# Hybrid decoder block on one core: the output projection's second and third chained products run one branch group later, the sums of activations come on every second step, and the second resident weight tile is asked for later

## The chip, the cores and the metric

The kernel runs on one core of one Trainium2 chip. The metric is the device time of one execution in microseconds (us); lower is better. The time before is 1326.16 us, the median of 3 runs (1325.57 to 1326.43).

## What is computed

One decoder block over 256 tokens of width 2048: an input projection, a dilated-window attention branch and a gated-MLP branch, a gated merge of the two, an output projection, a layer norm, a feed-forward layer of width 8192 and a second layer norm. The change touches the stage between the two branches and the output projection:

```python
y_a = jnp.einsum('bse,ed->bsd', attn, w_proj_a)
y_b = jnp.einsum('bse,ed->bsd', gmlp, w_proj_b)
merged = jax.nn.sigmoid(ga) * y_a + jax.nn.sigmoid(gb) * y_b
return jnp.einsum('bsd,de->bse', merged, w_out)
h = layer_norm(ALPHA * h + mix, ln1_gain[layer], ln1_bias[layer])
```

## The kernel before, in words

**Weights and precision.** Every weight matrix is read once, as chunks of 512 rows by 512 columns (1 MB, a `raw` tile of 4 x 512 per partition; three such buffers, loads issued from SP, L145). A chunk is used in two **pieces** of 128 x 1024. Each piece is split into a rounded part `hi` (a copy on ACT, L188) and a remainder `lo` (a subtraction on DVE, L157); TensorE (PE) multiplies with both. When the `lo` of a chunk's last piece has been written, the load of the chunk three places on is issued (L162).

**Steps.** The program is a list of steps in the order in which PE does them, one piece to a step. Six split buffers (the ring) hold pieces ahead of PE: at the emission of step s (`emit_splits`, L170; loop at L979) the split of the piece of step s + 5 is issued, into the buffer that step s - 1 has just left. So on ACT and DVE, which work in the order of issue, a split stands five steps ahead of its matmuls. In each step the order of issue is: the split; the hi and lo of finished activations (`rounds`); one or two pending finishing operations (`later`); the step's matmuls and, at the end of a group, its evacuations; then what `at` has hung on that step.

**Groups.** `pa` and `pb` are the branch groups: 512 columns of `w_pa` or `w_pb`, four steps each ("ws" mode, L252 and L254). At the end of one, four halves are copied from PSUM on ACT (`halves`, L273) and added on DVE (L277). After pb, DVE multiplies and adds for the gated merge (L486, L489), and hi and lo of the merged activations follow (L93, L94). "as" groups (L240 to L242) are quarters of the output projection in plain form, two steps to a chunk.

**Products.** For half of the output projection's columns, seven products P1 to P7 over 512 x 512 blocks take the place of eight ("sum" mode, L212 to L214, two steps of six matmuls each; the results are added up in `collect`, L684). Four of them use a **resident tile** that stays in SBUF: the first (`tiles["b", 0]`) is loaded once and, after each of P1, P5 and P6, changed in place: when the `lo` of the product's second piece is written, `held_add` (L632) issues from POOL a DMA that adds another weight block to it. So P1, P5, P6 and P4 are chained. The second resident tile (`tiles["b", 1]`, used by P7) is made by `held_load(uo, 1)` (L620): a plain load from POOL (L623) and, once that has landed, a DMA that adds a second block (L625). It lies on the buffer `A1`, which the merged activations of group 1 hold until the sums below have read them. Each such DMA moves 1 MB, and POOL issues its DMAs in program order.

**Sums of activations.** P5, P6, P7 and P3 take sums and differences of activations. `sum_of_acts` (L567) makes them in four parts k = 0 to 3: four DVE operations into `cb` (L575 to L578), then hi and lo (`ca`, L93 and L94) in the next step's `rounds`. P5's second step needs parts 2 and 3.

**The order around the change** (L844 to L861): pa0 pb0 pa1 pb1 pa2 P1 pb2 P5 pa3 P6 pb3, then the plain group of columns 1024 to 1535 in four chunks c0 to c3 with products between them: c0 P7 c1 P4 c2 P3 c3 P2. The sums are hung on P1's second step and the three steps that follow it; `held_load(uo, 1)` on P5's first step. After pb3, `start_residual` (L496) issues two loads of 1 MB from POOL, the residual rows `y`.

In the texts below, step 0 is the first step of pb2. The steps before the change are then: pb2 0 to 3, P5 4 and 5, pa3 6 to 9, P6 10 and 11, pb3 12 to 15, c0 16 and 17, P7 18 and 19, c1 20 and 21, P4 22 and 23. "P7a" and "P7b" are the first and second piece of P7, and so on for others.

Of the kernel before, what the change touches and what calls it, by code (L numbers as in the profile page):

```python
# [26 lines left out]
G = 8  # L27
# [44 lines left out]
def block_kernel(ctx: ExitStack, tc: tile.TileContext, xT, x, w_in, rel_bias, lnv_g, lnv_b, wsT, b_sp,  # L72
# [25 lines left out]
    chunks, pieces, steps = [], [], []  # L98
# [30 lines left out]
    def add_step(piece, part, first=False, last=False):  # L129
        pieces[piece]["uses"] += 1  # L130
        steps.append((piece, part, first, last))
        return len(steps) - 1

    def add_group(g, sizes=None):
        hs = add_pieces(g, sizes)
        for h in hs:
            add_step(h, "all", h == hs[0], h == hs[-1])
# [162 lines left out]
    tiles = {}  # L300
# [171 lines left out]
    def ev_ya(g):  # L472
        def fin(ot, s):
            gt = tiles["G", g]
            nc.vector.tensor_tensor(gt[:, 0, ot, :], gt[:, 0, ot, :], s, op=ALU.mult)

        def ev(ot, p):
            later.append((fin, ot, halves(p)))
        return ev

    def ev_yb(g):
        def fin(ot, s):
            if g == 0 and ot == 0:
                tiles["merged"] = quads("merged", [f"S1{i}" for i in range(4)])
            gt, d = tiles["G", g], tiles["merged"][g][:, ot, :]
            nc.vector.tensor_tensor(s, s, gt[:, 1, ot, :], op=ALU.mult)  # L486

            q = kept(ot) if g == 0 else gt[:, 0, ot, :] if g == 1 else s
            nc.vector.tensor_tensor(q, s, gt[:, 0, ot, :], op=ALU.add)  # L489
            rounds.append((hilo, d[:, :S], d[:, S:], q))  # L490

        def ev(ot, p):
            later.append((fin, ot, halves(p)))
        return ev
# [72 lines left out]
    def sum_of_acts(tags, ot, q):  # L567


        if ot == 0:  # L570
            for i in range(2):
                tiles["ca", i] = big.tile([P, 2, NCT, 2, P], F32R, name="ca", tag=tags[i])
        q0, t0, t1 = tiles["q", ot], slice(0, P), slice(P, S)
        cb = work.tile([P, 4, P], F32, name="cb", tag="pt")
        nc.vector.tensor_tensor(cb[:, 0], q0[:, t1], q[:, t1], op=ALU.subtract)  # L575
        nc.vector.tensor_tensor(cb[:, 2], q0[:, t0], q0[:, t1], op=ALU.subtract)
        nc.vector.tensor_tensor(cb[:, 1], cb[:, 0], q0[:, t0], op=ALU.subtract)
        nc.vector.tensor_tensor(cb[:, 3], q[:, t0], cb[:, 1], op=ALU.add)  # L578
        for i in range(2):
            d = tiles["ca", i][:, :, ot]  # L580
            rounds.append((hilo, d[:, :, 0], d[:, :, 1], cb[:, 2 * i:2 * i + 2]))
# [34 lines left out]
    def out_unit():  # L616
        return SimpleNamespace(w=w_out, row=0, act=lambda r, k: tiles["merged"][r][:, k, :],
                               tags=("S5", "A1"), acc="A0", key="out", scale=ALPHA)
# [176 lines left out]
    def quad(key):  # L795
        return lambda k: tiles[key][k // 4][:, k % 4, :]
# [5 lines left out]
    def at(s, f, *a):  # L802
        side.setdefault(s, []).append((f, a))
# [32 lines left out]
    uo = out_unit()  # L836
    prods = products(uo)

    def add_product(name):
        hs = prods[name]()  # L840
        for h in hs:
            add_step(h, "all", h == hs[0], h == hs[-1])

    at(len(steps) + 8, held_load, uo, 0)  # L844
    for i in range(4):
        add_group(Group(w_pa, i * CW, 8, quad("attnT"), "ws", ev_ya(i)))
        if i >= 2:
            add_product(("P1", "P6")[i - 2])
        if i == 2:
            for k in range(4):  # L850
                at(len(steps) - 1 + k, lambda k=k: sum_of_acts(("S6", "W"), k, tiles["G", 1][:, 0, k, :]))
        add_group(Group(w_pb, i * CW, 8, quad("gmlpT"), "ws", ev_yb(i), after=start_residual if i == 3 else None))
        if i == 2:
            at(len(steps), held_load, uo, 1)
            add_product("P5")

    g = Group(w_out, 2 * CW, 16, quad("merged"), "as", ev_out(2))
    for c, name in enumerate(("P7", "P4", "P3", "P2")):
# [169 lines left out]
```

## Time and profile before

| | before |
|---|---|
| median of 3 runs | 1326.16 us |
| the profiled execution's own time | 1326.2 us |
| its span | 1324.5 us |
| PE busy | 1312.9 us (99%) |
| DVE busy | 939.0 us (71%) |
| ACT busy | 691.0 us (52%) |
| POOL busy | 51.7 us (4%) |
| DMA | 288.83 MB, mean 218 GB/s |
| mean granted TensorE clock | 0.998 of full |

The profiled execution took 1326.2 us, 1.7 us more than its span, the time that the trace covers. An engine is busy when an instruction of it runs; matmuls are pipelined, so a matmul's listed duration (0.39 us for 512 columns) is longer than the distance to the next one (0.23 us). In a timeline a bracket at the end of a row gives the idle time of the engine just before it and what ended it.

### The profile page before, as it was taken

How to read it: one execution, taken by the hardware profiler on the slowest of the kernel's cores; microseconds unless marked ns; L12 is line 12 of the kernel's file. 1: busy time of each engine (PE TensorE's matmuls, PEld its weight loads, DVE VectorE, ACT ScalarE, POOL GpSimd, SP SyncE). 2: the span in 40 equal slices, each digit the busy share in tenths (PEclk: the TensorE clock that was granted, in tenths of full speed). 3: DMA queues.
4: the chain of work that ended last, by engine and by line, in shares of the span. 5: the costliest groups of instructions: out<-in, count | busy, mean ns of one | idle time of the engine just before them, and what ended most of it. 6: DMA issues, size and time to landing. Idle time of an engine off the chain costs nothing. (4 is left out here: it accounts for less than half of the span.)

```text
span 1324.5 us, 17423 instructions
## 1 busy us (share of the span) xinstructions
PE 1312.9 (99%) x6832; PEld 1111.0 (84%) x6832; DVE 939.0 (71%) x1426; ACT 691.0 (52%) x938; POOL 51.7 (4%) x57
## 2 busy tenths in 40 slices
PE   9999999999999999999999999999999999999998
PEld 6888888888888888889888888888888888888886
DVE  6554678565545689788769768678677796786776
ACT  4444465454544556545545366455555564555641
POOL 0000000000000001000000100010000000100000
PEclk9999999999999999999999999999999999999999
DMA  9866545546555569772874988987887879978561
GB/s 321 289 195 206 176 137 182 191 160 222 191 191 190 187 169 291 244 230 71 283 255 148 284 219 289 248 242 247 217 280 229 237 242 251 252 224 236 178 254 64
DMA packets 140003, 288.83 MB, mean 218 GB/s; under 512 B 5256, under 2 KB 7824, under 8 KB 139024
## 3 DMA queue, kind: packets, MB, share of 16 engines
q1 hardware_dynamic: 120592, 240.26, 53.5%
q0 software_dynamic: 19184, 47.20, 16.8%
q8 instruction: 53, 0.87, 0.3%
q10 hardware_dynamic: 144, 0.26, 0.1%
q14 instruction: 30, 0.25, 0.1%
HBM read 285.59 MB, written 2.11 MB: 217 GB/s over the span
## 5 line engine op out<-in xcount | busy, mean ns | idle before, releaser
L157 DVE TENSOR_TENSOR w<-raw,w 128x1024 fp32r<-128x1024 f32 (+1 forms) x438 | 529.2, 1218 | 300.8 <-ACT w L188 299.7
L188 ACT ACTIVATE w<-raw 128x1024 fp32r<-128x1024 f32 (+1 forms) x438 | 456.7, 1053 | 411.8 <-PE mm L254 289.7
L252 PE MATMUL mm<-hT,w 128*128 128x512 f32 x960 | 339.4, 394 | 0.8 <-DVE sum L277 0.8
L252 PE MATMUL mm<-xs,w 128*128 128x512 f32 x896 | 315.7, 395 | 0.0
L254 PE MATMUL mm<-hT,w 128*128 128x256 f32 x1024 | 276.0, 279 | 0.0
L254 PE MATMUL mm<-xs,w 128*128 128x256 f32 x896 | 250.0, 279 | 0.0
L252 PEld LDWEIGHTS mm<-hT,w 128*128 128x128 f32 x960 | 180.0, 187 | 44.3 <-DVE sum L277 1.1
L252 PEld LDWEIGHTS mm<-xs,w 128*128 128x128 f32 x896 | 167.9, 187 | 39.5
L254 PEld LDWEIGHTS mm<-hT,w 128*128 128x128 f32 x1024 | 188.0, 188 | 2.7
L254 PEld LDWEIGHTS mm<-xs,w 128*128 128x128 f32 x896 | 168.0, 187 | 0.2
L242 PE MATMUL mm<-w,a 128*128 128x512 f32 (+1 forms) x328 | 128.1, 390 | 0.0
L241 PE MATMUL mm<-w,a 128*128 128x512 f32 (+1 forms) x328 | 128.0, 390 | 0.0
L240 PE MATMUL mm<-w,a 128*128 128x512 f32 (+1 forms) x328 | 127.8, 390 | 0.0
L157 DVE TENSOR_TENSOR w<-held,w 128x1024 fp32r<-128x1024 f32 x70 | 85.6, 1223 | 39.3 <-ACT w L188 38.9
L188 ACT ACTIVATE w<-held 128x1024 fp32r<-128x1024 f32 x70 | 73.9, 1058 | 64.7 <-PE mm L242 26.6
L240 PEld LDWEIGHTS mm<-w,a 128*128 128x128 f32 x328 | 61.8, 188 | 14.3
L242 PEld LDWEIGHTS mm<-w,a 128*128 128x128 f32 x328 | 61.7, 188 | 14.0
L241 PEld LDWEIGHTS mm<-w,a 128*128 128x128 f32 x328 | 61.8, 188 | 13.9
L240 PE MATMUL mm<-w,xs 128*128 128x512 f32 x120 | 49.4, 412 | 0.3 <-ACT w L188 0.3
L241 PE MATMUL mm<-w,xs 128*128 128x512 f32 x120 | 47.7, 397 | 1.3 <-DVE w L157 1.3
L277 DVE TENSOR_TENSOR sum<-mm,half 128x256 f32<-128x256 f32 x136 | 48.9, 418 | 0.0
L242 PE MATMUL mm<-w,xs 128*128 128x512 f32 x120 | 47.6, 397 | 0.0
(193 smaller groups left out, 1512.8 us busy)
## 6 DMA issues: line engine op xcount, KB each, us to landing
raw<-in_w_ff_dram SPq DMA_DIRECT2D x116, 1024.0 KB, 6.5
raw<-in_w_in_dram SPq DMA_DIRECT2D x68, 1024.0 KB, 5.1
held<-in_w_ff_dram POOLq DMA_DIRECT2D x36, 1024.0 KB, 8.5
raw<-in_w_out_dram SPq DMA_DIRECT2D x14, 1024.0 KB, 5.4
raw<-in_w_pa_dram SPq DMA_DIRECT2D x8, 1024.0 KB, 5.1
raw<-in_w_pb_dram SPq DMA_DIRECT2D x8, 1024.0 KB, 5.1
held<-in_w_out_dram POOLq DMA_DIRECT2D x6, 1024.0 KB, 8.5
raw<-in_w_in_dram SPq DMA_DIRECT2D x6, 512.0 KB, 7.2
```

The source lines that it names most:

```text
L157: nc.vector.tensor_tensor(h["lo"], sl, f32(h["hi"]), op=ALU.subtract)
L188: nc.scalar.activation(h["hi"], source(h), AF.Copy)
L240: nc.tensor.matmul(p, ah, hi[:, kk, cs], start=first and kk == 0, stop=False)
L241: nc.tensor.matmul(p, ah, lo[:, kk, cs], start=False, stop=False)
L242: nc.tensor.matmul(p, al, hi[:, kk, cs], start=False, stop=last and kk == n - 1)
L252: nc.tensor.matmul(p, hi[:, kk, ws_], av, start=st, stop=False)
L254: nc.tensor.matmul(p[:, :S], lo[:, kk, ws_], av[:, :S], start=False, stop=en)
L277: nc.vector.tensor_tensor(s, p[:, :S], t, op=ALU.add)
```

## The change

The order becomes pa2 P1 pb2 pa3 P5 pb3 P6, then c0 P7 c1 P4 c2 P3 c3 P2 as before: P5 moves behind pa3 and P6 behind pb3. The sums of activations are hung on P1's second step (step -1) and on steps 1, 3 and 5. `held_load(uo, 1)` is issued at step 11, the second step of pb3. The steps after the change: pb2 0 to 3, pa3 4 to 7, P5 8 and 9, pb3 10 to 13, P6 14 and 15, c0 16 and 17, P7 18 and 19. No instruction is added or removed.

```diff
@@ -845,14 +845,14 @@
     for i in range(4):
         add_group(Group(w_pa, i * CW, 8, quad("attnT"), "ws", ev_ya(i)))
         if i >= 2:
-            add_product(("P1", "P6")[i - 2])
+            add_product(("P1", "P5")[i - 2])
         if i == 2:
             for k in range(4):
-                at(len(steps) - 1 + k, lambda k=k: sum_of_acts(("S6", "W"), k, tiles["G", 1][:, 0, k, :]))
+                at(len(steps) - 1 + 2 * k, lambda k=k: sum_of_acts(("S6", "W"), k, tiles["G", 1][:, 0, k, :]))
         add_group(Group(w_pb, i * CW, 8, quad("gmlpT"), "ws", ev_yb(i), after=start_residual if i == 3 else None))
-        if i == 2:
-            at(len(steps), held_load, uo, 1)
-            add_product("P5")
+        if i == 3:
+            at(len(steps) - 3, held_load, uo, 1)
+            add_product("P6")
```

## Rows read from the trace of the kernel before

**Rows 1.** The page: span and part 1, busy time of each engine.
```profile
span 1324.5 us, 17423 instructions
PE 1312.9 (99%) x6832; PEld 1111.0 (84%) x6832; DVE 939.0 (71%) x1426; ACT 691.0 (52%) x938; POOL 51.7 (4%) x57
```

**Rows 2.** Timeline of PE, 498 to 537 us: start, duration, engine, line, operation.
```profile
498.97 0.40 PE L212 MATMUL aux<-w,ca 128*128 128x512 f32 x1
...
502.23 0.50 PE L214 MATMUL aux<-w,ca 128*128 128x512 f32 x1 [0.53 <-DVE ca L94]
502.57 0.40 PE L252 MATMUL mm<-attnT,w 128*128 128x512 f32 x1
...
513.77 0.40 PE L212 MATMUL aux<-w,ca 128*128 128x512 f32 x1
...
533.50 0.40 PE L212 MATMUL aux<-w,ca 128*128 128x512 f32 x1
...
536.31 0.39 PE L240 MATMUL mm<-w,merged 128*128 128x512 f32 x1
```

**Rows 3.** Timeline of DVE, 500 to 508 us.
```profile
500.62 1.22 DVE L157 TENSOR_TENSOR w<-raw,w 128x1024 fp32r<-128x1024 f32 x1
501.76 0.75 DVE L94 TENSOR_TENSOR ca<-cb,ca 128x256 fp32r<-128x256 f32 x2
...
505.45 0.42 DVE L486 TENSOR_TENSOR sum<-sum,gate 128x256 f32<-128x256 f32 x1
...
507.71 0.42 DVE L486 TENSOR_TENSOR sum<-sum,gate 128x256 f32<-128x256 f32 x1
```

**Rows 4.** Timeline of POOL, 493 to 523 us.
```profile
493.25 1.29 POOL L632 DMA_DIRECT2D held<-in_w_out_dram  x1 [14.90 <-DVE w L157]
501.00 0.78 POOL L623 DMA_DIRECT2D held<-in_w_out_dram  x1 [6.47 <-DVE cb L578]
508.07 1.26 POOL L625 DMA_DIRECT2D held<-in_w_out_dram  x1 [6.29 <-DMA held<-in_w_out_dram]
510.02 1.27 POOL L632 DMA_DIRECT2D held<-in_w_out_dram  x1 [0.69 <-DVE w L157]
```

**Rows 5.** Tile held, issues at 493.3, 501.0, 508.1, 510.0: instruction and its landing.
```profile
L632 POOL DMA_DIRECT2D held<-in_w_out_dram x1: 1288/1288/1288, 493.3 to 493.3; - x1
DMA to landing us min/median/max: 8.4/8.4/8.4
...
DMA to landing us min/median/max: 6.8/6.8/6.8
...
DMA to landing us min/median/max: 8.9/8.9/8.9
...
L632 POOL DMA_DIRECT2D held<-in_w_out_dram x1: 1271/1271/1271, 510.0 to 510.0; - x1
DMA to landing us min/median/max: 14.2/14.2/14.2
```

**Rows 6.** Timeline of ACT, 519 to 529 us.
```profile
519.83 1.06 ACT L188 ACTIVATE w<-held 128x1024 fp32r<-128x1024 f32 x1
...
525.25 1.06 ACT L188 ACTIVATE w<-raw 128x1024 fp32r<-128x1024 f32 x1 [1.78 <-PE mm L254]
526.22 0.82 ACT L273 ACTIVATE half<-mm 128x256 f32<-128x256 f32 x2
...
528.36 1.05 ACT L188 ACTIVATE w<-raw 128x1024 fp32r<-128x1024 f32 x1
```

**Rows 7.** Busy time in 502 to 504 us: PE, PEld, DVE, ACT, POOL, clock, DMA, GB/s.
```profile
502.00:504.00 2.00, 1.77 (x10) 1.54 (x11) 1.84 (x6) 1.06 (x2) 0.00 (x0) 1.00 1.07 420
```

**Rows 8.** Timeline of ACT, 767 us (feed-forward stage), a wait for a resident tile.
```profile
767.14 1.06 ACT L188 ACTIVATE w<-held 128x1024 fp32r<-128x1024 f32 x1 [9.84 <-DMA held<-in_w_ff_dram]
```

**Rows 9.** Timeline of PE, 768 to 770 us, the matmuls of that tile.
```profile
768.65 0.39 PE L212 MATMUL aux<-w,ca 128*128 128x512 f32 x1
769.51 0.50 PE L213 MATMUL aux<-w,ca 128*128 128x512 f32 x1 [0.48 <-DVE w L157]
```

**Rows 10.** Tile held, the adding DMA issued at 746.7 us: its landing.
```profile
DMA to landing us min/median/max: 12.5/12.5/12.5
```

**Rows 11.** Busy time in two stretches near the end; columns as in Rows 7.
```profile
1316.00:1318.00 2.00, 0.53 (x2) 0.00 (x0) 1.45 (x3) 1.84 (x6) 0.00 (x0) 1.00 0.00 0
1318.00:1320.00 2.00, 1.35 (x2) 0.30 (x2) 1.94 (x4) 0.53 (x3) 0.00 (x0) 0.82 0.15 59
```

## The prediction

> **What bounds the kernel now.** I read the page first: PE is busy 1312.9 of 1324.5 us [rows 1], so a change that removes no matmul can win only PE's idle time, and any wait that it puts before a matmul is paid in full. Next I read PE's timeline through the stage of the change, where the reader should compare the lengths of like steps. A product is 12 matmuls: P7 runs from 533.50 to 536.31, 2.81 us. P5, the same 12 matmuls, runs from 498.97 to 502.57, 3.60 us [rows 2]. It loses 0.79 us because its last matmul waits for the remainder `ca` of the sums' fourth part. DVE's timeline shows why: it wrote a weight remainder from 500.62 and only then, from 501.76, the last `ca` [rows 3]. Those 0.79 us are all that this stage has to give. Then I read POOL's timeline and the landings, for the tiles that the change moves: each resident tile is a chain of 1 MB DMAs in POOL's order, 6.8 us for the plain load and 8.4 to 14.2 us for an adding one [rows 4, 5].
>
> **The gain.** After the change the fourth part of the sums is hung on step 5 and its `ca` comes in step 6; P5's second step is 9. At 2.81 us a step that is over 7 us of room where there was none, so the wait goes: -0.79 us. The four parts keep their work, now two steps apart. pa3 comes two product steps sooner, its raw loads in the old order three chunks ahead; I cost that at nothing, covered by the five steps of split pieces. Without that cover it would cost what a load is late.
>
> **PE's new timetable, without stalls.** pb2 ends at 498.97 as before. pa3 takes 502.57 to 513.77 = 11.20 us [rows 2], so it ends at 510.17; P5 ends at 512.98; pb3 at 524.18; P6 at 526.99. P7 starts where it did, less the gain: 533.50 - 0.79 = 532.71.
>
> **The first resident tile.** P5b's split goes into the buffer left at 498.97, behind the four halves of pb2. Like those of pb3, where a split starts at 528.36 after halves from 526.22 [rows 6], they take about 2.1 us; with 1.06 for `hi` and 1.22 for `lo` [rows 3, 6] P5's add is issued near 503.8. It lands 8.4 to 8.9 us later [rows 5], near 512.3. P6a's split is due at 511.6 and waits 0.7 us on ACT, which PE, over four steps behind it, does not see. P6b's split needs the buffer that P5 leaves at 512.98; behind P6a and the copy of P5's result, `hi` ends near 515.0 and `lo` near 516.2. So P6's add is issued at **516.4**, against 510.02 before [rows 4].
>
> **The second resident tile: the step that decides.** Before, its load was issued at 501.00, ahead of P6's add; its own add followed at 508.07 and landed at 508.07 + 8.9 = 517.0 [rows 4, 5], and P7a's split, at 519.83, did not wait [rows 6]. After, `held_load` stands behind P6's add on POOL: P6b's remainder is issued at step 10, the load at step 11. POOL reaches it only at 516.4 + 1.27 = **517.7**. Its buffer `A1` is long free by then; what holds it is the instruction ahead of it. Behind it on POOL wait its own add and the two residual loads, which the residual sum needs only after c3.
>
> How long the tile takes now has no row of its own. The least is the old pair of landings, load 6.8 and add 8.9, as if nothing were ahead: 517.7 + 15.7 = 533.4, with the issue of the second about 0.3 later 533.7. But the load queues behind P6's add. In the trace two adding DMAs 1.95 us apart landed at 517.0 and 524.2 [rows 4, 5], so they were served one after the other. P6's add lands at 516.4 + 8.6 = 525.0 (8.6 lies between the 8.4 and 8.9 of [rows 5]); the load then needs between 2.5 us (1 MB at the 420 GB/s of [rows 7]) and 7.2 us (the distance of those two landings). I take 3.5, nearer the short end because a plain copy is the quicker kind: 528.5. The add is issued at 528.8 and lands 8.6 us later: **T = 537.4**. With 7.2 for the load, or with the 12.5 us that an add took in the feed-forward stage [rows 10], T is 541.
>
> **What a landing at T costs PE.** P7a's split is due when PE leaves step 12, at 521.4, so ACT stands for 16 us, and DVE behind it. The nearest row is the feed-forward stage: there ACT stood 9.84 us for a resident tile, went on at 767.14, and the product's second matmul, which needs `lo`, started at 769.51, 2.4 us after it. PE had reached that product at 768.65 and lost 0.63 us (0.86 between two matmuls instead of 0.23) [rows 8, 9]. So five steps of cover are worth about 9 us of such a wait, and here the wait is some 6.5 us longer.
>
> After T the work that ACT and DVE hold must be done in order. ACT: P7a's `hi` to T + 1.15, the four halves of pb3, which stand between P7a and P7b as two splits with halves between them do at 525.25 and 528.36 [rows 6], then P7b's `hi` to about T + 4.2. DVE: P7a's `lo` to T + 2.4, four sums, P7b's `lo` to T + 5.4, and then rounds of one remainder, one gated merge and one activation remainder, 2.26 us each (505.45 to 507.71 [rows 3]): `lo` of c1 at T + 7.3 and T + 9.5, of P4 at T + 11.8 and T + 14.1. PE: P7a ends at T + 3.6, P7b at T + 6.6, c1 (waiting 0.5 us for its first `lo`) at T + 12.7, P4 at T + 15.5, and from there it runs at its own pace. Without a stall P4 would end at 532.71 + 2.81 + 5.62 + 2.81 = 543.95. The cost is T + 15.5 - 543.95 = T - 528.45: **8.95 us** for T = 537.4, 5.2 us for 533.7, 12.6 us for 541.
>
> Nothing behind this pays it back: PE is the bound to the end [rows 1].
>
> **The clock.** PE will stand idle some 6 us before P7. In the trace the granted clock falls only at the end: after 2 us in which PE was busy 0.53 us it is 1.00, and over the next 2 us 0.82, a fall from 2.4 to 1.2 GHz within that stretch [rows 11]. A fall before P7 would double the spacing of its matmuls, 12 x 0.23 = 2.8 us at most for P7; I add nothing, since P7 and c1's start wait for remainders anyway, which would hide most of it. The Trainium skill ("TensorE: Matmul & The Clock Gate", Part 1) says that the clock halves after idleness and returns only after sustained work; the trace agrees with the fall, with the 0.82. By that rule alone, with P7 unhidden, the sum would be 2.8 us higher.
>
> **The sum.** 1326.2 (the profiled execution, span 1324.5 and 1.7 around it, level with the median 1326.16) - 0.79 + 8.95 = **1334.4 us**.
>
> **Rivals.**
> - *The wait goes and nothing takes its place.* 1326.2 - 0.8 = 1325.4, no change that can be told (about 0.2%, 2.7 us, is what a measurement of this kernel can tell). It needs the tile by 532.94 - 2.4 = 530.5 at the latest, the second matmul of P7 less the 2.4 us of [rows 8, 9], that is a load issued by about 514.5 even with the old landings. For it: PE is hidden from a 9.84 us wait elsewhere. Against it: POOL's order. 0.11.
> - *The load does not queue behind P6's add.* T = 533.7, cost 5.25: 1330.7. Against it are the serial landings of [rows 5]. 0.20, inside the forecast's sign.
> - *Transfers share the DMA engines.* If raw loads run against the tile's add, it takes the 12.5 us of [rows 10] and T is 541: 1326.2 - 0.8 + 12.6 = 1338.0. ACT's stand speaks against it, since no `lo` is written and so few raw loads are issued. The Trainium skill ("DMA: Bandwidth & Descriptors", Queues, rings and completion order) says that an engine takes turns between its queues packet by packet, which is this rival's mechanism; no row here shows the turns themselves. 0.17.
> - *A wait elsewhere goes with it*, faster by over 2.7 us: the stage has 0.79 us of idle to give, so only a change of pace of the matmuls could do that. 0.03.
>
> **Numbers.** The forecast with T near 537, 0.49; queue not shared 0.20; shared engines 0.17; nothing but the gain 0.11; faster 0.03. Slower by over 0.2% is 0.49 + 0.20 + 0.17 = 0.86, within 0.2% 0.11, faster 0.03. The range starts at 1329.0, T = 532.0 (1.7 us under the least pair of landings), and reaches to 1340.0, the shared engines with part of the clock's 2.8 us; it leaves out the two cases without a stall.
>
> **What would show it.** Right: P5 lasts 2.81 us; POOL issues P6's add near 516 and the second tile's load at once behind it, its add near 529; ACT shows one wait of some 16 us for a resident tile of `w_out`; PE idles about 6 us before P7's first matmul, about 1 us before its second, and over 1 us at P7b; the rest of the trace is shifted by some 8 us. Wrong: P7a's split finds its tile landed, or the load is issued before P6's add, or PE regains the loss before the layer norm.

## The result and the profile after

The changed kernel takes 1338.74 us, the median of 4 runs (1337.72 to 1339.37), against 1325.98 us for the kernel before in the same comparison (4 runs, 1325.57 to 1326.43): 1.0095 times as long, 95% interval 1.0078 to 1.0113. That is 12.8 us more, where 8.2 were forecast (1334.4); the range, 1329.0 to 1340.0, holds it. The profiled execution of the changed kernel took 1337.72 us, its span is 1336.0 us, 11.5 us longer than the span before [rows 1].

The page, span and part 1, of the changed kernel:

```profile
span 1336.0 us, 17425 instructions
PE 1315.0 (98%) x6832; PEld 1112.1 (83%) x6832; DVE 937.8 (70%) x1426; ACT 690.3 (52%) x938; POOL 51.8 (4%) x57
```

The work is the same: each engine's count of instructions is that of [rows 1], and the two more of the first line are none of theirs. PE's idle time went from 11.6 to 21.0 us. Its busy time rose by 2.1 us, because most of P7 ran at the lower clock: from 544 to 546 us the granted clock (third number from the right, columns as in [rows 7]) was 0.50, that is 1.2 GHz.

```profile
544.00:546.00 2.00, 2.00 (x6) 1.31 (x4) 1.54 (x4) 2.00 (x3) 0.00 (x0) 0.50 0.53 221
```

Where PE stands idle is seen in its timeline, which answers to [rows 2]:

```profile
510.09 0.40 PE L212 MATMUL aux<-w,ca 128*128 128x512 f32 x1
...
512.88 0.39 PE L252 MATMUL mm<-gmlpT,w 128*128 128x512 f32 x1
...
532.39 0.39 PE L242 MATMUL mm<-w,merged 128*128 128x512 f32 x1
542.13 0.80 PE L212 MATMUL aux<-w,ca 128*128 128x512 f32 x1 [9.35 <-ACT w L188]
543.39 0.80 PE L213 MATMUL aux<-w,ca 128*128 128x512 f32 x1 [0.47 <-DVE w L157]
...
548.24 0.39 PE L240 MATMUL mm<-w,merged 128*128 128x512 f32 x1
```

The first two rows are the first matmul of P5 and the first behind it: 2.79 us, without the wait of before. Then P7: PE has done c0 by 532.6 and stands 9.35 us until the first `hi`, and again before the second matmul for the first `lo`. ACT, answering to [rows 6], and POOL, answering to [rows 4], show whose wait it is:

```profile
514.43 1.05 ACT L188 ACTIVATE w<-held 128x1024 fp32r<-128x1024 f32 x1
...
515.86 1.06 ACT L188 ACTIVATE w<-held 128x1024 fp32r<-128x1024 f32 x1
...
541.02 1.06 ACT L188 ACTIVATE w<-held 128x1024 fp32r<-128x1024 f32 x1 [21.23 <-DMA held<-in_w_out_dram]
```

```profile
502.90 1.29 POOL L632 DMA_DIRECT2D held<-in_w_out_dram  x1 [24.63 <-DVE w L157]
519.06 1.25 POOL L632 DMA_DIRECT2D held<-in_w_out_dram  x1 [14.87 <-DVE w L157]
519.81 1.29 POOL L623 DMA_DIRECT2D held<-in_w_out_dram  x1
532.49 1.26 POOL L625 DMA_DIRECT2D held<-in_w_out_dram  x1 [11.38 <-DMA raw<-in_w_out_dram]
```

The two splits at 514.43 and 515.86 are P6's; P6's add follows at 519.06. Only then, 0.75 us later and with no wait of its own, POOL comes to the second tile's load (L623), which before was issued at 501.00. The landings of the issues between 517 and 520 us (the add 9.0, the load 12.4) and of the tile's own add at 532.49, answering to [rows 5]:

```profile
DMA to landing us min/median/max: 9.0/10.7/12.4
```

```profile
DMA to landing us min/median/max: 8.5/8.5/8.5
```

The profile names a load of `raw` as what released L625, but that load, issued from SP at 521.7, landed only near 532.7. L625 came 0.3 us after the landing of its own tile's plain load, 519.81 + 12.4 = 532.2, as it did before the change (508.07, after 507.8).

So the tile is complete at 532.49 + 8.5 = 541.0, 21 us after the last split that ACT could do, and ACT takes it up at 541.02.

### The profile page after: what moved, and what is told of

It is laid out like the page before. It is cut to its first block, busy times and chain, and to the rows that moved or that the text cites. A ratio compares the mean times of both kernels' runs of the same rounds, so it can differ in the third digit from the quotient of the medians.

```text
span 1336.0 us, 17425 instructions
## 1 busy us (share of the span) xinstructions
PE 1315.0 (98%) x6832; PEld 1112.1 (83%) x6832; DVE 937.8 (70%) x1426; ACT 690.3 (52%) x938; POOL 51.8 (4%) x57
## 4 chain that ended last, share of the span: by engine, by line
PE 90%; DMA 4%; DVE 4%; ACT 1%; issue 1%; SPq 0%; ACTq 0%; DVEq 0%
PE mm L252 34%; PE mm L254 17%; PE mm L241 9%; PE mm L242 9%; PE mm L240 9%; PE aux L213 3%; PE aux L214 3%; PE aux L212 3%; DVE w L157 2%; DMA held<-in_w_ff_dram 1%; DMA raw<-in_w_out_dram 1%; PE mm L257 1%; ACT w L188 1%; DMA held<-in_w_out_dram 1%; DMA raw<-in_w_in_dram 1%
## 5 line engine op out<-in xcount | busy, mean ns | idle before, releaser
L212 PE MATMUL aux<-w,ca 128*128 128x512 f32 x112 | 45.2, 404 | 9.4 <-ACT w L188 9.4
L240 PE MATMUL mm<-w,xs 128*128 128x512 f32 x120 | 49.5, 412 | 0.1
L241 PE MATMUL mm<-w,xs 128*128 128x512 f32 x120 | 47.7, 397 | 1.3 <-DVE w L157 1.3
```

Of the source, the lines that this page charges most:

```text
L212: nc.tensor.matmul(p, ah, hi[:, kk], start=first and kk == 0, stop=False)
L240: nc.tensor.matmul(p, ah, hi[:, kk, cs], start=first and kk == 0, stop=False)
L241: nc.tensor.matmul(p, ah, lo[:, kk, cs], start=False, stop=False)
```

## The experiments

Two theories stood at the start. Mine: the whole loss is the landing of the second resident tile, which is late because on POOL its load stands behind P6's add. Against it: the load's late step as such, the moved products, or the sums on every second step. Besides, the size of the forecast was off by 4.6 us, and the clock had been costed at nothing.

**1. The load two steps earlier.** One number of the change, so that the load stands ahead of P6's add on POOL:

```diff
-            at(len(steps) - 3, held_load, uo, 1)
+            at(len(steps) - 5, held_load, uo, 1)
```

> The changed kernel with one number altered: the second resident tile is asked for at step 9 instead of 11, the last step at which it still stands ahead of P6's add on POOL. My theory (the loss comes from standing behind P6's add): the load is issued near 507.3, when the sums' fourth part has been read, its add lands near 524, ACT waits some 4 us for it (covered), PE does not wait at P7: 1325.2 us, 0.8 under the kernel before. Rival (the load is late because its step is late): two steps are 5.6 us of PE's time, so 1338.7 - 5.6 = 1333.1. Rival (moving the products or the sums costs it): 1338.7.

Measured: 1325.27 us (11 runs) against 1325.91 before, 0.9993 (0.9985 to 1.0002). POOL in this run:

```profile
503.08 1.29 POOL L632 DMA_DIRECT2D held<-in_w_out_dram  x1 [24.62 <-DVE w L157]
507.74 0.78 POOL L623 DMA_DIRECT2D held<-in_w_out_dram  x1 [3.37 <-DVE cb L578]
516.37 1.26 POOL L625 DMA_DIRECT2D held<-in_w_out_dram  x1 [7.86 <-DMA held<-in_w_out_dram]
519.23 1.27 POOL L632 DMA_DIRECT2D held<-in_w_out_dram  x1 [1.60 <-DVE w L157]
```

Two steps, 5.6 us of PE's time, move the load by 12 us, because in front of it there is no longer an instruction that waits for P6's remainder. Its add landed 10.8 us after 516.37, 3 us later than expected. ACT waited 7.3 us for the tile, until 527.24, where 4 were expected, and PE showed no wait at all between 440 and 600 us. The span is 0.9 us under the one before, P5's 0.8. This is the version that keeps the change's gain; the gain is too small to tell from no change.

**2. The load late, nothing else.** The kernel before, with its load put at step 11:

```diff
-            at(len(steps), held_load, uo, 1)
+            at(len(steps) + 7, held_load, uo, 1)
```

> The kernel before with only the load moved: the second resident tile asked for at step 11; products and sums stay. P6's add is then issued near 510.0 and the load at once behind it. My theory: the tile lands near 531, ACT stands 11 us for P7a; the first of P7's matmuls is just covered, and the work held back on ACT and DVE costs PE about 2 us by P4: 1328.2. Rival (the late load by itself is the whole loss): 1338.7. Rival (the late load is harmless while P6 is early): 1326.0.

Measured: 1331.82 us, 1.0038 (1.0025 to 1.0050). Neither rival: a late load costs something even with P6 early, and less than half of what it costs behind the moved P6. The forecast of 1328.2 was low by two terms, seen here:

```profile
535.45 0.50 PE L212 MATMUL aux<-w,ca 128*128 128x512 f32 x1 [2.02 <-ACT w L188]
536.71 0.71 PE L213 MATMUL aux<-w,ca 128*128 128x512 f32 x1 [0.76 <-DVE w L157]
...
538.50 0.63 PE L214 MATMUL aux<-w,ca 128*128 128x512 f32 x1
538.93 0.63 PE L212 MATMUL aux<-w,ca 128*128 128x512 f32 x1
```

```profile
536.00:538.00 2.00, 1.29 (x3) 1.08 (x4) 2.00 (x3) 2.00 (x5) 0.00 (x0) 0.71 1.01 426
538.00:540.00 2.00, 2.00 (x6) 1.53 (x5) 2.00 (x5) 0.42 (x3) 0.00 (x0) 0.50 0.03 12
```

The tile landed at 534.2, 3 us later than expected: its add, issued at 522.22, took 12.0 us. Two raw loads from SP were under way beside it (issued at 518.6 and 521.6, landed 7.9 and 10.8 us later); in the changed kernel, where the tile's add took 8.5 us, none was. And the spacing of P7's matmuls is 0.43 us instead of 0.23, with a granted clock of 0.71 and then 0.50; PE had been idle for 2.0 us and, one matmul later, for 0.8.

**3. The sums back on four successive steps**, the rest of the change kept:

```diff
-                at(len(steps) - 1 + 2 * k, lambda k=k: sum_of_acts(("S6", "W"), k, tiles["G", 1][:, 0, k, :]))
+                at(len(steps) - 1 + k, lambda k=k: sum_of_acts(("S6", "W"), k, tiles["G", 1][:, 0, k, :]))
```

> The changed kernel with the sums of activations back on four successive steps, -1 to 2. My theory: the load stands behind P6's add as before, P6's add comes within 2 us of the 519.06 of the changed kernel, so 1336.5 to 1339. Rival (the spreading of the sums holds DVE back and is the loss): 1325.5.

Measured: 1338.83 us, 1.0089 (1.0073 to 1.0104). The sums' places don't make the loss. P6's add was issued at 521.31, 2.2 us later than in the changed kernel, a little outside the 2 us expected. And the places are not without effect: PE waited 2.35 us for DVE near 500 us, and then only 7.2 instead of 9.4 us before P7. The earlier wait is taken off the later one, as long as the tile does not land later too: here ACT took it up 1.6 us later, and the profiled span is 2.2 us longer (1338.2 against 1336.0), though the medians are level. What the wait costs without that cover is run 7.

**4. Without the tile's second DMA.**

```diff
-        if i == 1:
+        if i == 1 and u.key == "ff":
             nc.gpsimd.dma_start(tiles["b", 1], block(u, 1, 1), accum_op=ALU.add)
```

> The changed kernel without the second adding DMA of the second resident tile of the output projection (the result is then not the reference's: one weight block is missing from P7). It shows what a landing some 8.8 us earlier is worth. My theory (PE pays T less about 528.5): the tile is there at 532.2, PE idles under 1 us before P7, the clock does not fall, cost about 3.7 us: 1329.3 to 1330.0. Rival (most of the loss is a fixed price of the late order, not of the landing): over 1334.

Measured: 1328.59 us (10 runs), 1.0019 (1.0010 to 1.0028). This is 0.7 us under the expected 1329.3 to 1330.0. With the tile taken up 9.3 us earlier the median is 10.2 us shorter and the profiled span 9.3 (1326.7): the loss follows the landing, and no fixed price of the order is left to see. ACT waited 11.6 us here and PE's first loss at P7 is under 1 us:

```profile
532.97 0.39 PE L212 MATMUL aux<-w,ca 128*128 128x512 f32 x1
534.09 0.50 PE L213 MATMUL aux<-w,ca 128*128 128x512 f32 x1 [0.73 <-DVE w L157]
```

**5. The plain load from SP instead of POOL.**

```diff
-        nc.gpsimd.dma_start(tiles["b", i], block(u, 0, i))
+        eng = nc.sync if (u.key, i) == ("out", 1) else nc.gpsimd
+        eng.dma_start(tiles["b", i], block(u, 0, i))
```

> The changed kernel with the plain load of the second resident tile issued from SP instead of POOL, so that it doesn't queue behind P6's add; its own add stays on POOL. My theory: the load is issued near 515.6, when SP is free, and lands near 524; its add is issued at once, but is served behind P6's add and lands near 535, 6 us before the 541 of the changed kernel: 1332.5 to 1333.5. Rival (queueing in the DMA engines is worth nothing, the order of issue alone decides): within 1 us of 1338.7.

Measured: 1335.12 us (1333.75 to 1336.11), 1.0066 (1.0052 to 1.0080). The direction holds; the saving is 3.6 us where some 5.7 were expected. POOL and ACT:

```profile
519.11 1.25 POOL L633 DMA_DIRECT2D held<-in_w_out_dram  x1 [14.87 <-DVE w L157]
524.07 1.27 POOL L626 DMA_DIRECT2D held<-in_w_out_dram  x1 [3.70 <-DMA held<-in_w_out_dram]
```

```profile
536.89 1.06 ACT L188 ACTIVATE w<-held 128x1024 fp32r<-128x1024 f32 x1 [17.06 <-DMA held<-in_w_out_dram]
```

Issued from SP at 515.98, 3.8 us earlier than from POOL, the load landed 7.8 us later, although P6's add was under way; from POOL it took 12.4. But P6's add, issued at 519.11, then took 11.3 us instead of 9.0:

```profile
DMA to landing us min/median/max: 11.3/11.3/11.3
```

It landed at 530.4, and the tile's own add, issued at 524.07 while P6's was still moving, took 12.7 us instead of 8.5. So the load came 8.4 us earlier and the tile only 4.2. On POOL's queue each transfer waited for the one ahead; beside each other, from SP and POOL, the load did not wait, and P6's add lost 2.3 us. Two raw loads from SP shared this stretch as well. The Trainium skill ("DMA: Bandwidth & Descriptors", SWDGE vs HWDGE vs iDMA) says that transfers issued from GpSimd and from SP feed different queues of the DMA engines, between which an engine takes turns; the 7.8 us of the load and the 11.3 us of P6's add beside it agree.

**6 and 9. PE kept busy in the gap.** The changed kernel with matmuls added before P7, into the bank that P7 overwrites (n = 36, then 43):

```diff
+            if first and h["chunk"] is None and h["held"] == ("b", 1) and "kept_busy" not in state:
+                state["kept_busy"] = True
+                m = tiles["merged"][0][:, 0, :]
+                for _ in range(n):
+                    nc.tensor.matmul(p, m[:, :P], m, start=True, stop=True)
```

> The changed kernel with 36 matmuls of 512 columns added on PE in the gap before P7 (8.5 of the 9.5 us that PE idles), into the bank that P7's first matmul then overwrites. They keep PE busy and cost nothing if they end before the tile's first hi. My theory (the lower clock is mostly hidden behind the remainders that P7 waits for): the clock stays at 2.4 GHz, P7 takes about 5.5 us instead of 6.1: 1338.1. Rival (the clock costs P7's 12 matmuls a doubled spacing, 2.8 us): 1336.

> The changed kernel with 43 instead of 36 matmuls of 512 columns added before P7 (10.1 us, the whole of the gap and 0.5 us of the wait for P7's first remainder). With 36 a gap of 2.2 us was left, and the granted clock fell all the same. My theory: no gap over 1.5 us is left, the clock stays at 2.4 GHz, P7 takes about 5 us from its first matmul instead of 6.1, and the time is 0.7 us under the changed kernel's: 1338.0. Rival (the lower clock costs more than P7 shows): 1336. Rival (matmuls in the gap hold up the transfer of the tile, as the 0.8 us longer landing with 36 suggests): 1340 to 1341.5, with a clock of 1.00.

Measured: 1341.36 us with 36 (1.0114, 1.0100 to 1.0128) and 1340.23 us with 43 (1.0105, 1.0088 to 1.0122). The first missed: the filling ended 2.2 us before P7, and the clock fell in what was left (0.61 and 0.50 granted from 544 to 548 us). With 43 it stayed up; the timeline of PE and the stretch of P7's second half in that run:

```profile
532.73 9.91 PE L214 MATMUL aux<-merged 128*128 128x512 f32 x43
543.75 0.50 PE L217 MATMUL aux<-w,ca 128*128 128x512 f32 x1 [1.11 <-ACT w L188]
545.01 0.50 PE L218 MATMUL aux<-w,ca 128*128 128x512 f32 x1 [0.76 <-DVE w L157]
...
546.77 0.50 PE L217 MATMUL aux<-w,ca 128*128 128x512 f32 x1 [0.32 <-ACT w L188]
548.03 0.50 PE L218 MATMUL aux<-w,ca 128*128 128x512 f32 x1 [0.76 <-DVE w L157]
```

```profile
546.00:548.00 2.00, 0.95 (x3) 0.20 (x2) 1.53 (x3) 1.66 (x2) 0.00 (x0) 1.00 0.03 12
```

At a full clock P7 only waits more, for the same `hi` and `lo` of its second piece (0.32 and 0.76 us): the remainders pace it, not the matmuls. P7 ended half a microsecond sooner after the tile's take-up by ACT than in the changed kernel (6.66 us instead of 7.22), and by P4's first matmul even that was gone: 12.80 us after the take-up, against 12.83. In run 4 it is 12.81 at a full clock, in run 5 12.82 at the lower one. So the lower clock cost the changed kernel next to nothing. Where it held for all 12 matmuls of P7, in runs 3 and 6, it is 13.5, 0.7 us more.

The third rival of the run with 43 is the one whose number came out. Its reason accounts for half of it: the tile's add took 9.3 and 9.9 us in these two runs instead of 8.5, and in the run with 43 ACT took the tile up 1.6 us later, while the profiled span is 2.9 us longer than the changed kernel's. That the added matmuls slow the transfer is suggested by two runs and not shown.

**7. The products moved, the sums as before, the load early (step 4).**

```diff
-                at(len(steps) - 1 + 2 * k, lambda k=k: sum_of_acts(("S6", "W"), k, tiles["G", 1][:, 0, k, :]))
+                at(len(steps) - 1 + k, lambda k=k: sum_of_acts(("S6", "W"), k, tiles["G", 1][:, 0, k, :]))
...
-            at(len(steps) - 3, held_load, uo, 1)
+            at(len(steps) - 10, held_load, uo, 1)
```

> Only the products moved: P5 behind pa3 and P6 behind pb3, the sums back on four successive steps, the load early at step 4. The run with the sums put back showed PE waiting 2.3 us for DVE at the start of pa3, beside the wait for the tile. My theory: the wait for the tile is gone, that for DVE stays, P5's 0.8 us are won: 1326.0 - 0.8 + 2.3 = 1327.5. Rival (the sums' places cost nothing once the tile is there in time): 1325.2.

Measured: 1329.33 us (10 runs), 1.0019 (1.0009 to 1.0028), 1.8 us over the forecast. PE and the granted clock at the start of pa3:

```profile
503.08 0.80 PE L252 MATMUL mm<-attnT,w 128*128 128x512 f32 x1 [2.36 <-DVE sum L277]
503.67 0.42 PE L254 MATMUL mm<-attnT,w 128*128 128x256 f32 x1
503.89 0.63 PE L252 MATMUL mm<-attnT,w 128*128 128x512 f32 x1
504.32 0.41 PE L254 MATMUL mm<-attnT,w 128*128 128x256 f32 x1
```

```profile
502.00:504.00 2.00, 0.92 (x3) 0.83 (x4) 2.00 (x7) 1.03 (x3) 0.00 (x0) 0.75 0.88 341
504.00:506.00 2.00, 2.00 (x8) 1.71 (x8) 1.54 (x3) 0.45 (x1) 0.00 (x0) 0.50 0.00 0
```

The wait for DVE was the 2.4 us that run 3 showed. Behind it a pair of matmuls takes 0.64 us instead of the 0.35 of full clock until 506.2, some 1.5 us more. So the spreading of the sums is worth about 4 us once the products are moved (run 1 took 1325.27; its load is at another step, but in neither run did PE wait for the tile): four parts in a row hold up the sums of pb2's halves on DVE, whose banks pa3 needs.

**8. Run 2 with 7 matmuls added before P7.**

> The kernel before with the load alone at step 11, and 7 matmuls of 512 columns added before P7, where PE idled 2 us and the granted clock fell to 1.2 GHz during P7. My theory: here no halves stand between P7's two splits, so nothing hides the lower clock, and it is what that run lost beyond the landing: the clock stays up, P7 ends 1.9 us sooner: 1331.8 - 1.9 = 1329.9. Rival (the clock costs nothing here either): 1331.8.

Measured: 1330.75 us, 1.0034 (1.0021 to 1.0047). The clock stayed at 1.00 and P7 took 4.0 us (535.88 to 539.88) instead of 5.5; but the tile was taken up 0.4 us later than in run 2, and PE then met a wait of 0.5 us for a remainder in c2. So the profiled span is no shorter (1329.1 against 1328.9), the median is 1.1 us lower where 1.9 were expected, and the intervals overlap: what the clock cost run 2 in the end is not told apart from nothing.

## Why the prediction was right, and where it was short

**The mechanism** held at each step: P5's wait went (2.79 us instead of 3.60), POOL issued P6's add and the load at once behind it, ACT stood in one long wait, PE paid before P7's first and second matmul, and hardly anything was won back behind it: P4 ended 11.9 us later than before, the span 11.5. One sign did not come: at P7b PE lost about 0.3 us, not over 1. The rule "cost is T - 528.45, less the gain of 0.79", T being the tile's landing, was worked out from rows of the kernel before, a wait in the feed-forward stage first. Against the runs that keep the order of the products (ACT's take-up is up to 0.15 us after T, 0.1 is taken; span of before 1324.5; run 7, which lost its time in pa3, is left out):

| run | ACT takes the tile up | by the rule | span, difference |
|---|---|---|---|
| 1, load at step 9 | 527.24 | -0.8 (no cost, the gain alone) | -0.9 |
| 4, no second add | 531.72 | +2.4 | +2.2 |
| 5, load from SP | 536.89 | +7.6 | +7.5 |
| the change | 541.02 | +11.7 | +11.5 |
| 3, sums back | 542.66 | +13.3 | +13.7 |
| 9, 43 matmuls added | 542.64 | +13.3 | +14.4 |
| 6, 36 matmuls added | 543.13 | +13.8 | +15.6 |

So what a landing costs was sized right to 0.4 us in five runs, over a span of 15 us. The two runs with matmuls added lost more: 0.7 to 0.8 us of it stand in the feed-forward stage, where PE waited longer for a resident tile, and in run 6 another 0.7 in P7 at the lower clock. In the changed kernel two small errors inside the rule cancel: P7 ended at T + 7.2 instead of T + 6.6, its matmuls spaced by the lower clock, and c1 then did not wait the 0.5 us that I had put.

**What was short is T**: 541.0 instead of 537.4. The first term that failed is "P6's add is issued at **516.4**": it was issued at 519.06, 2.7 us later. I had put P6a's split right behind the landing of P5's add, at 512.3. In the trace it started at 514.43 and no transfer held it: P5's add, issued at 502.90, landed by 511.5. (My 503.8 for that issue is 0.45 more than its terms add up to; nothing hung on it.) On ACT the split stood behind the halves of pa3, and these waited for DVE:

```profile
510.56 0.91 ACT L273 ACTIVATE half<-mm 128x256 f32<-128x256 f32 x3
512.90 0.38 ACT L273 ACTIVATE half<-mm 128x256 f32<-128x256 f32 x1 [1.42 <-PE aux L213]
```

```profile
508.65 0.75 DVE L94 TENSOR_TENSOR ca<-cb,ca 128x256 fp32r<-128x256 f32 x2
...
512.39 1.41 DVE L277 TENSOR_TENSOR sum<-mm,half 128x256 f32<-128x256 f32 x4
```

There are three buffers for halves, and the fourth half goes on 0.5 us after DVE's sums begin. The profile names PE as the releaser here; in the kernel before, at the same distance (502.94 after 502.43), it names the sum. DVE was busy without a break from 503 to 513.8 us with pb2's gated merges, the remainders and the fourth part of the sums, which the change had put into that place. P6b's `lo` then stood behind a finishing operation on DVE, another 0.6 us that I had left out.

The second is what lies on the queue behind it. P6's add took 9.0 us where I had 8.6, and the load, "I take 3.5", landed 4.1 us behind it (528.1 to 532.2). I had looked for a raw load only beside the tile's own add. There was one beside these two transfers: issued from SP at 521.7, it took 11.0 us to land, where those issued at 497.4 and 515.5 took 5.1 and 5.5. That this sharing is the whole of the 1.0 us is not shown. The tile's own add, 8.5, was right. The median lies another microsecond above the profiled execution, and the runs scatter (1337.72 to 1339.37) about twice as far as those of before; whether it is the landing that scatters is not shown.

**The clock**, costed at nothing, cost about nothing (runs 4, 5 and 9), for the reason given: P7's pieces wait for remainders anyway. It is not free where no such wait follows: 1.5 us in run 7.

**The rivals.** "The wait goes and nothing takes its place" is what run 1 gives, 1325.27, and needed the load ahead of P6's add, as its condition said. In run 5 the load did not queue, and the time was 1335.12, not the 1330.7 of that rival, because the tile's own add then stood behind P6's. "Transfers share the DMA engines" named a T of 541 and 1338.0, nearer to the 1338.74 that came than my own sum, but it came by another way: the tile's add took 8.5 us, not 12.5; it was issued late. Its mechanism is seen on other transfers: P6's add beside the load in run 5, the tile's add beside raw loads in run 2.

## What to carry to other kernels

A DMA that waits for nothing itself is still as late as the instruction ahead of it on its queue: before moving a request to a later step, read what will then stand in front of it, when that is released, and add the transfers of the same queue that are still under way, and what other queues move beside them. An early-splitting engine five steps ahead hid waits of up to some 9 us here and then passed on every further microsecond, plus what it had left undone. When several moves are tied together, try each alone: here one number (the load's step) decided between 12.8 us lost and nothing lost.

## What the runs showed that was not expected

The clock can fall after a short idle of PE: after 2.36 us without a matmul in the middle of a stage in which PE had been busy all along, the granted clock was 0.75 and then 0.50 over the next 4 us, and 1.5 us were lost on top of the 2.4 (run 7). After gaps of 2.0 and 0.8 us it fell as well (run 2), and with the first of them filled to 0.65 us it stayed at 1.00 (run 8). The length of the gap alone does not tell when: in the changed kernel PE stood from 532.6 us, and the clock was 1.00 until 536, 0.86 from 536 to 538 and 0.50 after that. What sets the moment is not shown here.
